# Value products of a token tile in one row, and a block compression in one row over four column strips

## The chip, the cores and the metric

The kernel runs on one core of a Trainium2 chip. The metric is the device time of one execution in microseconds; a time of a kernel is the median of several runs.

## What is computed

A decoder trunk of two layers on 256 tokens of width 1024, batch 1, all in fp32. A layer normalises its input, projects it to 5472 columns, mixes the tokens in two ways (NSA and DSA), gates and adds the two, projects back and adds the residual; a SwiGLU FFN with 2816 hidden columns follows. What touches the change, cut down:

```python
def _compress(kv, pos_emb, w1, b1, w2, b2):      # keys and values of NSA, 15 blocks of 32 tokens
    blocks = kv[:, idx] + pos_emb[:, None, :]
    blocks = ...reshape(bsz, n_cmp, groups, CMP_BLOCK * hd)      # 2048 long
    hidden = jax.nn.gelu(blocks @ w1 + b1)                       # w1: 2048 x 128
    return hidden @ w2 + b2

# NSA, 8 heads in 2 groups: compressed, selected and window attention, gated and added
o_c = p_c @ vc;  o_s = p_s @ v_slc;  o_w = p_w @ v_win
out = g[:, :, 0] * o_c + g[:, :, 1] * o_s + g[:, :, 2] * o_w
# DSA, 8 heads: softmax over the 64 tokens that an indexer chose
o = masked_softmax(q @ k.T * ATTN_SCALE, chosen) @ v
```

## The kernel before

The tokens lie in two tiles of 128 (`i` = 0 and 1). Tensor-engine instructions are issued through the Tile framework, which orders them when the program is built: a planner with a simulated timeline gives each engine its next instruction, the earliest of the program among those that are ready. `tc.manual_schedule` fixes the order of the instructions inside one block for an engine.

Weights come through `weights` (lines 155 to 167): a load of up to 512 KB on SP's queue into one of five raw buffers, a rounding to fp32r on the scalar engine (line 164, `hi`), a subtraction on the vector engine (line 165, `lo`), each into one of four pairs of buffers. `mul3` (lines 169 to 175) makes three fp32r products of them for each tile. These wide products have 512 (or 280, 292, 256) columns.

In a layer the order of the program is: projection of the indexer, its scores and top-k (lines 381 to 453); projections for NSA (458 to 494); the compression (497 to 548); projections of DSA's queries, keys and values (551 to 560); `nsa(0)`, `nsa(1)`, `dsa(0)`, `dsa(1)` (570 to 683); four projections of the gates, with a tanh into `gates` (691 to 694); the two branches, NSA's first (733 to 740); the output projection and the FFN. As the planner takes what is ready, the gates' projections and the first branch products also run between the attention's instructions.

The compression multiplies blocks of 32 columns (15 blocks of two groups, padded) with `w1`. Keys and values (`kind`) and the two halves of a block (`half`) make four sums of 8 products each, which lie in four strips of 32 partitions of one PSUM bank `hp` (`tile_position=(0, q)`). A strip's products come one behind the other (lines 508 to 518). The weights come in eight loads of 256 KB through three buffers `w1`; in layer 0 the first three wait for the first projection, by a copy into a corner of the buffer (`after`). `hp` is copied (line 520), its halves are added (522), and the GELU and second products follow.

`softmax` (287 to 312) takes two score banks of a step, and gives each its probabilities, transposed by the tensor engine (line 280) and copied into a buffer `pt` (line 281), of which there are five. `nsa(i)` goes over its heads in steps of `per = 2 - i` (two steps for tile 0, four for tile 1), `dsa(i)` in one and two steps. A step has two `pt` buffers. `values` (602 to 610 and 644 to 651) multiplies a step's `pt` with the values, into 64 partitions of the bank `yv` for each of two heads in turn; with `LAG = 1` it is called for a step once the next step's softmax is in the program. Behind the steps of `nsa(i)` the compressed values are added (line 634), and `y_out` (565 to 568) takes the bank out for the branches.

`gb` is a buffer of 5632 columns. It holds `gates` (columns 0 to 4095), and behind them `pji`, later `dkT` and `vbd`. The same memory (`bigB`) holds the low halves `hl` of the FFN's hidden values at the end of a layer.

Of the kernel before, what the change touches and what calls it, by code (L numbers as in the profile page):

```python
# [9 lines left out]
F32 = mybir.dt.float32  # L10
# [6 lines left out]
P = 128  # L17
# [10 lines left out]
TAKEN = -3e38  # L28
TOPK = 64
WARM = 11  # L30
LAG = 1
HALF = (slice(0, 64), slice(64, 128))
PTB = 5


C_KCMP, C_VCMP, C_KSLC, C_VSLC, C_KWIN, C_VWIN, C_NG = 512, 640, 768, 896, 1024, 1152, 1280
# [43 lines left out]
def hybrid_trunk(ctx: ExitStack, tc: tile.TileContext, a: dict, out: bass.AP):  # L80
# [272 lines left out]
    for l in range(DEPTH):  # L353
# [19 lines left out]
        qs = one.tile([P, 2, 4, SEQ], F32R, tag="qs", name="qs")  # L373
        ikT = carve(ga, 5168, P)
        gates = carve(gb, 0, NT, 2 * D)
        pji = carve(gb, 4096, NT, 648)
        dkT = carve(gb, 4096, 4, SEQ)
        vbd = carve(gb, 5120, 8, 64)
# [115 lines left out]
            nc.vector.tensor_scalar(eg[:, i], eg[:, i], 1.0, None, ALU.add)  # L494


        hp = sc_bank()
        for kind, nm in ((0, "cmpk"), (1, "cmpv")):
            blk = work.tile([P, 16, 32], F32, tag="pr", name="blk", bufs=8)
            blk4 = blk.rearrange("p m (g c) -> p m g c", g=2)  # L500
            nc.vector.memset(blk4[:, :, :, 15:16].rearrange("p m g c -> p (m g) c"), 0.0)
            pos = (R_KP, R_VP)[kind] + 16 * l
            for half in range(2):
                src = kvP[:, kind].rearrange("p g (c m) -> p m g c", m=8)[:, :, :, half:half + 15]
                po = cols[:, pos + half * 8:pos + half * 8 + 8].unsqueeze(2).broadcast_to((P, 8, 15))
                for g in range(2):
                    nc.vector.tensor_add(blk4[:, half * 8:(half + 1) * 8, g, 0:15], src[:, :, g], po)
            for half in range(2):
                q = 32 * (2 * half + kind)
                for mq in range(2):  # L510
                    r0 = half * 1024 + mq * 512
                    w1 = work.tile([P, 4, P], F32, tag="w1", name="w1", bufs=3)
                    if l == 0 and kind == 0 and half + mq < 2:
                        after(w1[:, 0, 0:1], pji[:, 0, 0:1])
                    nc.sync.dma_start(w1, a[nm + "_w1"][l, r0:r0 + 512].rearrange("(m p) h -> p m h", p=P))
                    for m in range(4):
                        nc.tensor.matmul(hp[q:q + 32, 0:P], blk[:, half * 8 + mq * 4 + m], w1[:, m],  # L517
                                         start=mq == 0 and m == 0, stop=mq == 1 and m == 3, tile_position=(0, q))
        hs = work.tile([P, P], F32, tag="hs", name="hs", bufs=1)
        nc.vector.tensor_copy(hs, hp[:, 0:P])  # L520
        hT = sc_bank()
# [48 lines left out]
        def nsa(i):  # L570
            tok = slice(i * P, (i + 1) * P)
            nk = P * (i + 1)

            cb = sc_bank()
            for r in range(4):
                nc.tensor.matmul(cb[:, r * 32:(r + 1) * 32], qT[:, r, tok], kcbd.rearrange("p g c -> p (g c)"),
                                 start=True, stop=True)
            pc = work.tile([P, 8, 16], F32, tag="pc", name="pc")
            m8 = small.tile([P, 8], F32, tag="cm", name="cm")
            s8 = small.tile([P, 8], F32, tag="cs", name="cs")  # L580
            bias = cst[:, K_CB + 16 * i:K_CB + 16 * i + 16].unsqueeze(1).broadcast_to((P, 8, 16))
            ok = cst[:, K_C01 + 16 * i:K_C01 + 16 * i + 16].unsqueeze(1).broadcast_to((P, 8, 16))
            nc.vector.tensor_add(pc, cb[:, 0:128].rearrange("p (h c) -> p h c", h=8), bias)
            nc.vector.tensor_reduce(m8, pc, AX.X, ALU.max)
            nc.vector.tensor_sub(pc, pc, m8.unsqueeze(2).broadcast_to((P, 8, 16)))
            nc.scalar.activation(pc, pc, AF.Exp, scale=0.125)
            nc.vector.tensor_mul(pc, pc, ok)
            nc.vector.tensor_reduce(s8, pc, AX.X, ALU.add)
            nc.vector.tensor_scalar_max(s8, s8, 1e-30)
            nc.vector.scalar_tensor_tensor(s8.rearrange("p (r g) -> p r g", g=2),  # L590
                                           eg[:, i, 0:8].rearrange("p (g r) -> p r g", g=2), 1.0,
                                           s8.rearrange("p (r g) -> p r g", g=2), ALU.mult, ALU.mult)
            nc.vector.reciprocal(m8, s8)
            nc.vector.tensor_mul(pc, pc, m8.unsqueeze(2).broadcast_to((P, 8, 16)))
            pct = work.tile([P, 1, P], F32, tag="pct", name="pct")
            transpose_into(pct, [pc.rearrange("p h c -> p (h c)")])


            per = 2 - i
            yn = yv_bank()  # L600

            def values(r0, pts):
                for r in range(r0, r0 + per):
                    for kind, vcol in ((0, C_VSLC - C0), (1, C_VWIN - C0)):
                        for b in range(i + 1):
                            for g in range(2):
                                nc.tensor.matmul(yn[g * 64:(g + 1) * 64, r * P:(r + 1) * P],  # L607
                                                 pj[:, b, vcol + g * 64:vcol + g * 64 + 64],
                                                 pts[g][:, ((r - r0) * 2 + kind) * (i + 1) + b],
                                                 start=r == 0 and kind == 0 and b == 0, stop=False)  # L610

            done = []
            for r0 in range(0, 4, per):
                pts = []
                sbs = [sc_bank() for _ in range(2)]
                outs = [[sb[:, n * 256 * (i + 1):(n + 1) * 256 * (i + 1)] for n in range(per)] for sb in sbs]
                for r in range(r0, r0 + per):
                    for g in range(2):
                        score(outs[g][r - r0], qs[:, g, r, tok],
                              [t[g][:, 0:i + 1].rearrange("p b t -> p (b t)") for t in (kh, kl)])  # L620
                for g in range(2):
                    segs = []
                    for o in outs[g]:
                        ov = o.rearrange("p (b k t) -> p k b t", b=i + 1, k=2)
                        segs += [ov[:, 0], ov[:, 1]]
                    gate = eg[:, i, 8:24].rearrange("p (k g r) -> p g r k", k=2, g=2)[:, g, r0:r0 + per]
                    pts.append(softmax(segs, causal(i), gate))
                done.append((r0, pts))
                if len(done) > LAG:
                    values(*done.pop(0))  # L630
            for d in done:
                values(*d)
            for r in range(4):
                nc.tensor.matmul(yn[:, r * P:(r + 1) * P], vbd[:, 2 * r:2 * r + 2].rearrange("p g d -> p (g d)"),  # L634
                                 pct[:, 0], start=False, stop=r == 3)
            y_out(yn, 0, tok)

        def dsa(i):
# [1 line left out]
            nk = P * (i + 1)  # L640
            per = 512 // nk
            yd = yv_bank()

            def values(p0, pts):
                for p in range(p0, p0 + per):
                    for b in range(i + 1):
                        for e in range(2):
                            v0 = (2 * p + e) * 64
                            nc.tensor.matmul(yd[e * 64:(e + 1) * 64, p * P:(p + 1) * P], dv[:, b, v0:v0 + 64],  # L649
                                             pts[e][:, (p - p0) * (i + 1) + b], start=p == 0 and b == 0,  # L650
                                             stop=p == 3 and b == i)

            done = []
            for p0 in range(0, 4, per):
                pts = []
                sbs = [sc_bank() for _ in range(2)]
                for p in range(p0, p0 + per):
                    outs = [sb[:, (p - p0) * nk:(p - p0 + 1) * nk] for sb in sbs]
                    if i == 0:
                        for e in range(2):  # L660
                            nc.tensor.matmul(outs[e], dqT[HALF[e], p, 0:P], dkT[HALF[e], p, 0:P], start=True, stop=True)
                    else:
                        for e in range(2):
                            score(outs[e], [dqs[:, z, p] for z in (e, 2 + e)], dks[:, e, p])
                for sb in sbs:
                    segs = sb.rearrange("p (h b t) -> p h b t", h=per, t=P)
                    pts.append(softmax([segs[:, h] for h in range(per)], dbias[i], None))
                done.append((p0, pts))
                if len(done) > LAG:
                    values(*done.pop(0))  # L670
            for d in done:
                values(*d)
            y_out(yd, 4, tok)

        for i in range(NT):
# [197 lines left out]
```

## Time and profile before

| | us |
|---|---|
| median of 3 runs | 821.17 (820.97 to 821.17) |
| the profiled execution, whole | 821.0 |
| its span in the profile | 819.2 |
| tensor engine busy (PE) | 810.9 (99%) |
| vector engine busy (DVE) | 549.5 (67%) |
| scalar engine busy (ACT) | 461.3 (56%) |
| mean rate of the DMA | 171 GB/s |

PE is the tensor engine's multiplication, PEld its weight load, which lies beside it. A matmul's record starts with its first column and lasts until its last result, so records overlap, and the distance from one start to the next is what a matmul costs in a row. SPq is the queue on which the loads are issued. A line such as `73.22 2.40 PE L517 ... x24` says that 24 instructions of line 517 started from 73.22 us on and that the last one ended 2.40 us later.

### The profile page before, as it was taken

To read this page: it belongs to the slowest core of one execution; us is meant where nothing else is said; L and a number is where in the kernel's file an instruction comes from. 1 tells how busy PE (TensorE), PEld (TensorE's weight loads), DVE (VectorE), ACT (ScalarE), POOL (GpSimd) and SP (SyncE) were. 2 spreads that over 40 slices of the span, in tenths; PEclk is the share of its full clock that TensorE was granted. 3 is DMA by queue.
4 is the path that set the end of the run, shared out by engine and by line. 5 is a ranking of instruction groups with operands and counts; after the bars stand their busy time and mean duration, and the time that the engine had idled before them with its cause. 6 is when DMAs were issued, how large, how long until landed. Compare 5 with 4: busy or idle time off the path is not lost.

```text
span 819.2 us, 12201 instructions
## 1 busy us (share of the span) xinstructions
PE 810.9 (99%) x4437; PEld 679.2 (83%) x4437; DVE 549.5 (67%) x1201; ACT 461.3 (56%) x791; POOL 8.4 (1%) x18
## 2 busy tenths in 40 slices
PE   8999999999999999999999999999999999999997
PEld 7887888888888888988898888888888888889886
DVE  5799668887665555554577994889776556546445
ACT  6866358773655445444467644778556445444433
POOL 0100000000000000000000000000000000000000
PEclk9999999999999999999999999999999999999999
DMA  8955754125475664576376564542345665547651
GB/s 275 343 165 168 218 172 138 52 81 180 152 231 164 196 183 152 169 241 193 102 214 191 170 207 142 153 129 78 128 134 175 206 192 183 182 119 231 202 177 52
DMA packets 76332, 140.09 MB, mean 171 GB/s; under 512 B 5056, under 2 KB 24512, under 8 KB 76272
## 3 DMA queue, kind: packets, MB, share of 16 engines
q1 hardware_dynamic: 76032, 138.59, 54.2%
q0 software_dynamic: 240, 0.72, 0.4%
q8 instruction: 35, 0.57, 0.3%
q14 instruction: 25, 0.20, 0.1%
HBM read 138.24 MB, written 1.05 MB: 170 GB/s over the span
## 4 chain that ended last, share of the span: by engine, by line
PE 98%; DMA 1%; SPq 0%; ACT 0%; DVE 0%; issue 0%; POOLq 0%; ACTq 0%
PE mm L175 26%; PE mm L173 26%; PE mm L174 26%; PE tr L280 3%; PE sc L335 2%; PE sc L517 2%; PE yv L607 2%; PE yv L175 2%; PE yv L174 2%; PE yv L173 1%; PE tr L798 1%; PE yv L649 1%; DMA raw<-w_in 1%; PE tr L234 1%; PE yv L634 1%; PE sc L174 0%
## 5 line engine op out<-in xcount | busy, mean ns | idle before, releaser
L165 DVE TENSOR_TENSOR lo<-raw,hi 128x1024 fp32r<-128x1024 f32 (+3 forms) x264 | 301.7, 1148 | 159.2 <-ACT hi L164 155.4
L164 ACT ACTIVATE hi<-raw 128x1024 fp32r<-128x1024 f32 (+3 forms) x264 | 262.2, 1000 | 189.3 <-PE mm L175 129.0
L174 PE MATMUL mm<-lo,ah 128*128 128x512 f32 (+3 forms) x850 | 318.9, 375 | 0.0
L175 PE MATMUL mm<-hi,al 128*128 128x512 f32 (+3 forms) x850 | 318.6, 376 | 0.0
L173 PE MATMUL mm<-hi,ah 128*128 128x512 f32 (+3 forms) x850 | 317.5, 379 | 0.0
L175 PEld LDWEIGHTS mm<-hi,al 128*128 128x128 f32 x850 | 159.8, 188 | 28.4 <-issue 1.5
L174 PEld LDWEIGHTS mm<-lo,ah 128*128 128x128 f32 x850 | 160.1, 188 | 26.8 <-issue 0.3
L173 PEld LDWEIGHTS mm<-hi,ah 128*128 128x128 f32 x850 | 159.7, 188 | 27.1 <-ACT hi L164 0.3
L300 ACT ACTIVATE pr<-pr,mx 128x128 f32<-128x128 f32 (+1 forms) x96 | 42.7, 448 | 12.4 <-DVE mx L297 12.1
L174 PE MATMUL mm<-lo,hh 128*128 128x512 f32 x126 | 49.3, 391 | 0.0
L175 PE MATMUL mm<-hi,hl 128*128 128x512 f32 x126 | 49.1, 390 | 0.0
L173 PE MATMUL mm<-hi,hh 128*128 128x512 f32 x126 | 48.7, 395 | 0.0
L803 DVE TENSOR_TENSOR hl<-tr,hh 128x512 fp32r<-128x512 f32 (+1 forms) x24 | 15.5, 647 | 36.5 <-ACT hh L802 36.5
L802 ACT ACTIVATE hh<-tr 128x512 fp32r<-128x512 f32 (+1 forms) x24 | 13.5, 562 | 45.4 <-PE tr L798 45.4
L175 PEld LDWEIGHTS mm<-hi,hl 128*128 128x128 f32 x126 | 23.7, 188 | 4.9
L174 PEld LDWEIGHTS mm<-lo,hh 128*128 128x128 f32 x126 | 23.7, 188 | 4.1
L173 PEld LDWEIGHTS mm<-hi,hh 128*128 128x128 f32 x126 | 23.7, 188 | 4.2
L309 DVE TENSOR_SCALAR pr<-pr,c 128x128 f32<-128x128 f32 (+1 forms) x96 | 24.7, 316 | 0.6
L297 DVE CUSTOM_DVE_ANT_0 pr<-sc,cst 128x128 f32<-128x128 f32 (+1 forms) x64 | 19.0, 353 | 6.3 <-PE sc L335 6.0
L280 PE MATMUL tr<-cst,pr 128*128 128x128 f32 x144 | 20.7, 273 | 0.0
L789 ACT ACTIVATE sg<-mm,rstd 128x512 f32<-128x512 f32 (+1 forms) x24 | 15.7, 654 | 8.8 <-PE mm L175 8.6
L281 ACT COPY pt<-tr 128x512 f32<-128x512 f32 x32 | 17.6, 584 | 4.4 <-PE tr L280 4.4
(247 smaller groups left out, 800.3 us busy)
## 6 DMA issues: line engine op xcount, KB each, us to landing
raw<-w_in SPq DMA_DIRECT2D x72, 512.0 KB, 3.7
raw<-w_ffn_down SPq DMA_DIRECT2D x44, 512.0 KB, 4.4
raw<-w_ffn_gate SPq DMA_DIRECT2D x40, 512.0 KB, 4.5
raw<-w_ffn_up SPq DMA_DIRECT2D x40, 512.0 KB, 4.3
raw<-w_out SPq DMA_DIRECT2D x16, 512.0 KB, 4.1
raw<-w_in SPq DMA_DIRECT2D x16, 292.0 KB, 3.7
raw<-w_branch_nsa SPq DMA_DIRECT2D x16, 256.0 KB, 3.9
raw<-w_branch_dsa SPq DMA_DIRECT2D x8, 512.0 KB, 3.7
```

Of the source, the lines that this page charges most:

```text
L164: nc.scalar.activation(hi[:, 0:kt * n], raw[:, 0:kt * n], AF.Copy)
L165: nc.vector.tensor_sub(lo[:, 0:kt * n], raw[:, 0:kt * n], hi[:, 0:kt * n].bitcast(F32))
L173: nc.tensor.matmul(dst, xh, wh, start=first, stop=False)
L174: nc.tensor.matmul(dst, xh, wl, start=False, stop=False)
L175: nc.tensor.matmul(dst, xl, wh, start=False, stop=last)
L280: nc.tensor.transpose(tp[:, k * P:(k + 1) * P], piece, ident)
L281: nc.any.tensor_copy(dst, tp[:, 0:len(parts) * P].rearrange("p (k t) -> p k t", t=P))
L297: nc.vector.tensor_tensor_reduce(pr[:, h].rearrange("p (b t) -> p b t", t=P), v, b3, -0.125, 3.4e38, ALU.add, ALU.min, accum_out=mx[:, h:h ...
L300: nc.scalar.activation(pr[:, h], pr[:, h], AF.Exp, bias=mx[:, h:h + 1], scale=-1.0, accum_out=sm[:, h:h + 1])
L309: nc.vector.tensor_scalar_mul(pr[:, h], pr[:, h], c[:, h:h + 1])
L335: nc.tensor.matmul(o, u, v, start=n == 0, stop=n == 1)
L517: nc.tensor.matmul(hp[q:q + 32, 0:P], blk[:, half * 8 + mq * 4 + m], w1[:, m], start=mq == 0 and m == 0, stop=mq == 1 and m == 3, tile_pos ...
```

## The change

The value products of a token tile no longer follow each step: they stand in one block of fixed order behind the last softmax of the tile, from the last head pair to the first, the two strips in turn. `LAG` goes, and `pt` has eight buffers. The compression's 32 products stand in one block of fixed order too, in which the four strips take turns. Its weights come in four loads of 512 KB into the memory of `gates`, which is written later in the layer; the `w1` buffers go.

```diff
-LAG = 1
-PTB = 5
+PTB = 8
...
         gates = carve(gb, 0, NT, 2 * D)
+        w1s = [gb[:, z * 1024:(z + 1) * 1024].rearrange("p (m h) -> p m h", h=P) for z in range(4)]
...
         hp = sc_bank()
-        for kind, nm in ((0, "cmpk"), (1, "cmpv")):
+        blks = []
+        for kind in range(2):
             blk = work.tile([P, 16, 32], F32, tag="pr", name="blk", bufs=8)
...
-            for half in range(2):
-                q = 32 * (2 * half + kind)
-                for mq in range(2):
-                    r0 = half * 1024 + mq * 512
-                    w1 = work.tile([P, 4, P], F32, tag="w1", name="w1", bufs=3)
-                    if l == 0 and kind == 0 and half + mq < 2:
-                        after(w1[:, 0, 0:1], pji[:, 0, 0:1])
-                    nc.sync.dma_start(w1, a[nm + "_w1"][l, r0:r0 + 512].rearrange("(m p) h -> p m h", p=P))
-                    for m in range(4):
-                        nc.tensor.matmul(hp[q:q + 32, 0:P], blk[:, half * 8 + mq * 4 + m], w1[:, m],
-                                         start=mq == 0 and m == 0, stop=mq == 1 and m == 3, tile_position=(0, q))
+            blks.append(blk)
+        strips = [(half, kind) for half in range(2) for kind in range(2)]
+        for (half, kind), w1 in zip(strips, w1s):
+            if l == 0:
+                after(w1[:, 0, 0:1], pji[:, 0, 0:1])
+            src = a[("cmpk_w1", "cmpv_w1")[kind]][l, half * 1024:(half + 1) * 1024]
+            nc.sync.dma_start(w1, src.rearrange("(m p) h -> p m h", p=P))
+        with tc.manual_schedule(engines={nc.tensor.engine}):
+            for m in range(8):
+                for (half, kind), w1 in zip(strips, w1s):
+                    q = 32 * (2 * half + kind)
+                    nc.tensor.matmul(hp[q:q + 32, 0:P], blks[kind][:, half * 8 + m], w1[:, m],
+                                     start=m == 0, stop=m == 7, tile_position=(0, q))
...
-            def values(r0, pts):
...
                 done.append((r0, pts))
-                if len(done) > LAG:
-                    values(*done.pop(0))
-            for d in done:
-                values(*d)
+            with tc.manual_schedule(engines={nc.tensor.engine}):
+                for n, (r, kind, b, g) in enumerate((r, kind, b, g) for r in range(3, -1, -1) for kind in range(2)
+                                                    for b in range(i + 1) for g in (1, 0)):
+                    r0, pts = done[r // per]
+                    vcol = (C_VSLC, C_VWIN)[kind] - C0 + g * 64
+                    nc.tensor.matmul(yn[g * 64:(g + 1) * 64, r * P:(r + 1) * P], pj[:, b, vcol:vcol + 64],
+                                     pts[g][:, ((r - r0) * 2 + kind) * (i + 1) + b], start=n < 2, stop=False)
...
-            def values(p0, pts):
...
                 done.append((p0, pts))
-                if len(done) > LAG:
-                    values(*done.pop(0))
-            for d in done:
-                values(*d)
+            with tc.manual_schedule(engines={nc.tensor.engine}):
+                for p in range(3, -1, -1):
+                    p0, pts = done[p // per]
+                    for b in range(i + 1):
+                        for e in (1, 0):
+                            v0 = (2 * p + e) * 64
+                            nc.tensor.matmul(yd[e * 64:(e + 1) * 64, p * P:(p + 1) * P], dv[:, b, v0:v0 + 64],
+                                             pts[e][:, (p - p0) * (i + 1) + b], start=p == 3 and b == 0,
+                                             stop=p == 0 and b == i)
```

## Rows read from the trace of the kernel before

**Rows 1.** The page, busy time of the tensor engine.

```profile
PE 810.9 (99%) x4437; PEld 679.2 (83%) x4437; DVE 549.5 (67%) x1201; ACT 461.3 (56%) x791; POOL 8.4 (1%) x18
```

**Rows 2.** The page, chain that ended last, by engine.

```profile
PE 98%; DMA 1%; SPq 0%; ACT 0%; DVE 0%; issue 0%; POOLq 0%; ACTq 0%
```

**Rows 3.** Windows, layer 0: busy us (x) PE, PEld, DVE, ACT, POOL; clock; DMA share; GB/s.

```profile
95.00:100.00 5.00, 5.00 (x27) 4.16 (x26) 1.61 (x3) 3.00 (x5) 0.00 (x0) 1.00 0.60 178
...
165.00:170.00 5.00, 5.00 (x42) 4.33 (x41) 5.00 (x27) 4.77 (x19) 0.00 (x0) 1.00 0.65 213
170.00:175.00 5.00, 5.00 (x42) 4.13 (x41) 5.00 (x20) 3.06 (x11) 0.00 (x0) 1.00 0.38 105
```

**Rows 4.** Instructions of lines 517 and 607: durations, first and last start, shapes.

```profile
L517 PE MATMUL sc<-w,blk x128: 272/273/297, 73.2 to 496.5; 128*32 128x128 f32 x128
...
L607 PEld LDWEIGHTS yv<-pt,ga x192: 132/137/137, 134.4 to 577.1; 128*64 128x64 f32 x192
L607 PE MATMUL yv<-pt,ga x192: 272/273/324, 134.4 to 577.2; 128*64 128x128 f32 x192
```

**Rows 5.** Timeline of the tensor engine around compression groups of layer 0: start, length.

```profile
72.90 0.40 PE L174 MATMUL mm<-lo,ah 128*128 128x512 f32 x1
73.22 2.40 PE L517 MATMUL sc<-w,blk 128*32 128x128 f32 x24
75.55 0.50 PE L175 MATMUL mm<-hi,al 128*128 128x512 f32 x1
...
82.76 0.40 PE L175 MATMUL mm<-hi,al 128*128 128x512 f32 x1
83.08 1.94 PE L517 MATMUL sc<-w,blk 128*32 128x128 f32 x16
84.95 0.66 PE L280 MATMUL tr<-cst,dq 128*128 128x128 f32 x4
...
90.46 0.39 PE L174 MATMUL mm<-lo,ah 128*128 128x512 f32 x1
90.69 0.39 PE L175 MATMUL mm<-hi,al 128*128 128x512 f32 x1
91.01 1.06 PE L517 MATMUL sc<-w,blk 128*32 128x128 f32 x8
92.00 0.50 PE L173 MATMUL mm<-hi,ah 128*128 128x512 f32 x1
92.33 0.40 PE L174 MATMUL mm<-lo,ah 128*128 128x512 f32 x1
```

**Rows 6.** Timeline of the tensor engine around value groups of layer 0.

```profile
164.50 0.39 PE L174 MATMUL mm<-lo,ah 128*128 128x512 f32 x1
164.81 1.09 PE L607 MATMUL yv<-pt,ga 128*64 128x128 f32 x16
165.84 1.21 PE L335 MATMUL sc<-dks,dqs 128*128 128x256 f32 x8
...
173.65 1.09 PE L607 MATMUL yv<-pt,ga 128*64 128x128 f32 x16
...
176.50 0.50 PE L173 MATMUL mm<-hi,ah 128*128 128x512 f32 x1
...
186.43 1.09 PE L649 MATMUL yv<-pt,ga 128*64 128x128 f32 x14
```

**Rows 7.** Waits of SP's queue: total us, times, longest.

```profile
SPq L515 <- PE sc L517: 8.4, 10, 1.6
```

**Rows 8.** Windows early in layer 0 and early in layer 1.

```profile
20.00:25.00 5.00, 5.00 (x26) 4.20 (x25) 3.65 (x4) 3.57 (x7) 0.00 (x0) 1.00 1.03 400
...
410.00:415.00 5.00, 5.00 (x40) 4.83 (x38) 4.59 (x14) 4.26 (x13) 0.55 (x1) 1.00 0.53 157
...
420.00:425.00 5.00, 5.00 (x36) 4.79 (x36) 3.71 (x5) 3.68 (x6) 0.00 (x0) 1.00 0.98 316
```

**Rows 9.** Timeline, the last FFN product of layer 0.

```profile
409.69 0.39 PE L175 MATMUL yv<-spare,hl 128*128 128x512 f32 x1
```

More of the change, by code (lines that the diff above doesn't have):

```diff
@@ L600, in nsa @@
             yn = yv_bank()
-            def values(r0, pts):
[L603 to L610, printed above, removed]
             done = []
@@ L642, in dsa @@
             yd = yv_bank()
-            def values(p0, pts):
[L645 to L651, printed above, removed]
             done = []
```

## The prediction

> **What bounds the kernel now.** I read the page's busy times first, then the chain of work that ended last. The tensor engine is busy 99% of the span and the chain lies on it for 98% [rows 1, 2]: whoever takes work from that engine gains it, as long as the other engines keep up. So I ask of each edit what it takes from the tensor engine, and then, in the windows of 5 us, whether something else is close to full. It is in one place: between 165 and 175 us the vector engine is busy all of the time [rows 3], while from 95 to 100 us it is busy a third of it [rows 3]. The granted clock is 1.00 (2.4 GHz) in all these windows, and the change leaves no gap that would lower it.
>
> Then the timeline of the tensor engine around the lines that change. A fp32 product makes two passes: line 517 has 64 products in the program and 128 matmul records, line 607 has 96 and 192 [rows 4]. What the reader is to see there is that these small products come in groups between wide matmuls, and that a group costs more than its passes.
>
> **Compression, before.** A layer has 64 passes in five groups, of 24, 8, 16, 8 and 8. In the group of 16 the passes, all to one strip of 32 columns, follow at (1.94 - 0.27) / 15 = 0.11 us, 0.27 being the duration of the last [rows 4, 5]. Two wide matmuls in a row start 0.23 us apart (90.46 to 90.69) [rows 5]; so the cost of a group is the time from the start before it to the start behind it, less 0.23, plus what the next step is longer than usual (0.33 instead of 0.23 behind the group of 8; 0.06 where transposes follow). That gives 24: 2.65 - 0.23 + 0.13 = 2.55 (the two steps behind it are longer there); 16: 2.19 - 0.23 + 0.06 = 2.02; 8: 1.31 - 0.23 + 0.10 = 1.18 [rows 5]. With three groups of 8 a layer pays 2.55 + 2.02 + 3 x 1.18 = 8.1 us. Of a group some 0.34 us is the change of shape: about 0.1 on the way in, 0.1 out, and the rest the longer first steps.
>
> **Compression, after.** One row of 64 passes, in which consecutive products go to four different strips. How many strips run at once is not in the trace for four. For two it is: 16 value passes that alternate between two strips take 1.09 us, that is (1.09 - 0.27) / 7 = 0.117 a step for eight steps of two [rows 6], and nothing is lost against one strip. So the bounds are four at once, 16 steps, which is the cost of the present group of 16, 2.0 us; and two at once, 32 steps, 2.0 + 16 x 0.11 = 3.8 us. I take four, as two showed no loss. The saving is 8.1 - 2.0 = 6.1 us a layer, **12.1 us** in all; by the other bound 4.3 a layer, 8.7 in all. The start flags, the bank and the sums are as before; the row waits for both blocks, whose additions are the same instructions.
>
> **Value products.** The passes stay, as does their step. Between the first group of a layer at 134.4 us and the last at 186.4 there are eleven groups [rows 4, 6]; after the change there are four rows. A group of 16 costs 1.34 - 0.23 + 0.10 = 1.21 us between a wide matmul and a score [rows 6], and its eight steps 8 x 0.109 = 0.87; the remaining 0.34 is what a merged group saves. Seven groups fewer: 2.4 us a layer, 4.9 in all.
>
> What this adds is a wait: the first product of a row, of the last head pair, waits for the last softmax of the tile, and everything behind it on the tensor engine waits too; `y_out` waits for the whole row. Three of the four groups of heads of tile 1 move from 151 to 165 us to the row's end. In their place come projections of the gates and the first branch matmuls, which are the only work without a softmax ahead. They already run out: from 173.65 to 176.50 there is no wide matmul, only the value group, the compressed values and transposes [rows 6]. In that stretch the vector engine is full [rows 3], so its chain sets the pace and the tensor engine would idle. The gain here is bounded by 4.9 us from above; from below by three groups of 1.2 us a layer that move to the end and leave idle time behind, 3.6 against the 2.4 saved, so 2.4 us lost in both layers. But each of these groups now stands in front of the next scores and delays them by its 1.0 us (164.81 to 165.84) [rows 6]; that goes, and shortens the chain. I take half of the upper bound, **2.5 us**. Eight transposed-probability buffers instead of five are what the row of tile 1 needs (four steps of two); the next tile's copies wait until that row is through, as they now wait for its last group.
>
> **Loads.** The bytes stay: eight loads of 256 KB become four of 512 KB a layer, 2 MB. Gone are the waits of the load queue for line 517, 8.4 us in ten waits [rows 7]; the tensor engine did not wait for data in those places, so they bring nothing. New is when the 2 MB come. In layer 0 all four wait for the first projection and come at once, 1.25 MB more than now, near a stretch with the DMA engines full at 400 GB/s [rows 8]: 3 us of transfer, which the prepared weights (five raw, four split) should cover; I take 0, at most 1. In layer 1 the gates' memory is the one that held the FFN's low halves, so the loads wait for the last FFN product, at 409.69 us [rows 9], where the queue turns to the loads of the first projection. Those windows have DMA shares of 0.53 and 0.98 [rows 8]; 2 MB at 400 GB/s are 5.2 us more. What stands behind the four loads on the queue is late by up to that; split weights in hand cover most of it. I take **1 us lost**, bounds 0 and 3. The corner copies rise from three to four, one column each, on a vector engine with room.
>
> **Sum.** 12.1 + 2.5 - 1.0 = 13.6 us. The profiled execution took 821.0 us (span 819.2 and 1.8 around it), 0.2 below the median of 821.2; 821.2 - 13.6 = **807.6 us**.
>
> **Rivals.**
> Two strips at once. If a pass cannot start before the one ahead of it in the program, the second pass of a product, which waits for the first, holds back the next strip, and only two overlap: 8.7 + 2.5 - 1.0 = 10.2 saved, 811.0 us. Against it: by such an order the 16 value passes would need eight steps from the first start to the last, and (1.09 - 0.27) leaves room for seven of 0.117 [rows 6]. The Trainium skill states this order (TensorE: Matmul & The Clock Gate, "What overlaps and what doesn't": matmuls start and end strictly in program order, and a weight load overlaps only a matmul of another row group); by it the sum is this rival's. The trace does not agree with the second half either: 16 loads of 137 ns lie within 1.09 us, though all strips here use the same rows [rows 4, 6]. Chance 0.14.
>
> The fillers run out. All that the value rows save comes back as idle time of the tensor engine, and 1 us a layer of the compression with it: 12.1 - 2.0 - 1.0 = 9.1, 812.1 us. For it stands the full vector engine at 165 to 175 us [rows 3]. Chance 0.11.
>
> The row is broken. The fixed order holds within the row, but the planner may still put other work between its products; each break costs 0.34 us. With three breaks in each of ten rows 10 us are gone: 817 to 818 us. Chance 0.04. If everything cancels, no change: 0.03.
>
> Slower. The chain of softmaxes on the vector and scalar engines sets the pace from the top-k on, and the tensor engine is full only because it is handed filler. Then all that it saves, 8.5 us a layer, turns to idle time, and the late rows lengthen the chain: 64 passes instead of 16 before `y_out` of tile 1 are 24 steps, 2.6 us, and 32 instead of 14 at the last row are 0.9, so 3.5 us a layer; with 1 us of loads 821.2 + 7.0 + 1.0 = 829 us. It becomes slower than before once less than half of the 8.5 us gets through (4.0 / 8.5 = 0.47). Against it stands the vector engine's third from 95 to 100 us [rows 3]: the chain can start earlier there. Chance 0.05.
>
> **How the numbers follow.** The forecast case has 0.63. Its cases and the first three rivals are faster by more than 0.2% (1.6 us, about what a measurement here can tell): 0.63 + 0.14 + 0.11 + 0.04 = 0.92; the same 0.03; slower 0.05. The range goes from all gains in full with no loss, 821.2 - 12.1 - 4.9 = 804.2, to two strips, no gain from the values and 3 us of late loads: 821.2 - 8.7 + 3.0 = 815.5.
>
> **What would show it.** Right: one group of 64 passes a layer on line 517's products with about 1.9 us from first start to the end (3.6 for two strips), four value rows a layer, no tensor-engine idle behind loads after 410 us. Wrong: tensor-engine waits on the vector engine between 150 and 180 us, waits on loads after 410, or compression passes still 0.11 us apart one by one.

## The result, and the profile after

The changed kernel takes 806.36 us (median of 4 runs, 806.26 to 806.85), the kernel before 821.07 us beside it (820.77 to 821.17): a ratio of 0.982 with a 95% interval of 0.981 to 0.983, 14.7 us faster. 807.6 was forecast. The profiled execution took 806.85 us whole, 0.5 above its median, with a span of 805.1.

The page's first line and the head of its chain, which answer to [rows 1, 2]:

```profile
PE 796.1 (99%) x4437; PEld 670.4 (83%) x4437; DVE 544.1 (68%) x1196; ACT 462.6 (57%) x797; POOL 8.4 (1%) x18
...
PE 97%; DMA 2%; ACT 0%; SPq 0%; DVE 0%; issue 0%; POOLq 0%; ACTq 0%
```

The tensor engine has the same 4437 matmul records and is busy 14.8 us less (810.9 before): the gain is cheaper records, not fewer. And the DMA has risen from 1% to 2% of the chain; that is the price, below.

The tensor engine's timeline around the compression of layer 0 (start, length, as in [rows 5]; line numbers are those of the changed kernel, 172 to 174 being `mul3`):

```profile
72.70 0.40 PE L173 MATMUL mm<-lo,ah 128*128 128x512 f32 x1
73.03 0.41 PE L523 MATMUL sc<-gb,blk 128*32 128x128 f32 x2
73.36 0.50 PE L174 MATMUL mm<-hi,al 128*128 128x512 f32 x1
73.70 0.39 PE L172 MATMUL mm<-hi,ah 128*128 128x512 f32 x1
73.93 0.40 PE L173 MATMUL mm<-lo,ah 128*128 128x512 f32 x1
74.25 1.95 PE L523 MATMUL sc<-gb,blk 128*32 128x128 f32 x62
76.13 0.50 PE L174 MATMUL mm<-hi,al 128*128 128x512 f32 x1
76.47 0.40 PE L172 MATMUL mm<-hi,ah 128*128 128x512 f32 x1
```

Five groups have become one of 62 passes, with a small one of two ahead. From the first start to the last the 62 take 1.95 - 0.27 = 1.68 us, 15.4 steps of 0.109: four passes to a step. But the row is broken behind its first product (two passes), and three wide matmuls stand in between. By the prediction's rule for the cost of a group, with a next step of 0.34 us behind each, the 62 cost 2.20 - 0.23 + 0.11 = 2.08 us and the two 0.66 - 0.23 + 0.11 = 0.54. Layer 1 has the same groups.

The value rows of layer 0, which answer to [rows 6]; there are no others in the layer:

```profile
130.18 1.97 PE L631 MATMUL yv<-pt,ga 128*64 128x128 f32 x32
...
161.11 3.71 PE L631 MATMUL yv<-pt,ga 128*64 128x128 f32 x64
...
170.15 1.09 PE L666 MATMUL yv<-pt,ga 128*64 128x128 f32 x16
...
178.41 1.97 PE L666 MATMUL yv<-pt,ga 128*64 128x128 f32 x32
```

Windows over the attention of layer 0, columns as in [rows 3]:

```profile
145.00:150.00 5.00, 5.00 (x33) 4.20 (x34) 4.93 (x22) 5.00 (x14) 0.00 (x0) 1.00 0.01 2
150.00:155.00 5.00, 5.00 (x29) 4.29 (x28) 5.00 (x17) 4.70 (x17) 0.00 (x0) 1.00 0.54 161
155.00:160.00 5.00, 5.00 (x31) 4.38 (x29) 5.00 (x28) 5.00 (x14) 0.00 (x0) 1.00 0.64 216
...
165.00:170.00 5.00, 5.00 (x33) 4.38 (x32) 1.38 (x2) 1.56 (x3) 0.00 (x0) 1.00 0.05 20
170.00:175.00 5.00, 5.00 (x39) 4.13 (x38) 1.81 (x2) 3.65 (x5) 0.00 (x0) 1.00 0.02 3
```

The full stretch of the vector engine has moved some 15 us to the front, and from 165 to 175 us it now works for a third of the time. The tensor engine is busy for 5.00 of every 5 us throughout, at a clock of 1.00 (2.4 GHz): the fillers did not run out.

Now the loads. The load queue's timeline early in layer 1, and the chain there (start, us, what):

```profile
401.66 0.37 SPq L518 DMA_DIRECT2D gb<-cmpk_w  x1
402.07 0.58 SPq L518 DMA_DIRECT2D gb<-cmpv_w  x1
402.75 0.65 SPq L161 DMA_DIRECT2D raw<-w_in  x1
403.44 0.84 SPq L518 DMA_DIRECT2D gb<-cmpk_w  x1
404.38 1.34 SPq L161 DMA_DIRECT2D raw<-w_in  x1
405.76 0.56 SPq L518 DMA_DIRECT2D gb<-cmpv_w  x1
```

```profile
406.42 8.78 DMA raw<-w_in
415.31 1.07 ACT hi L163
416.40 1.24 DVE lo L164
417.68 0.50 PE mm L173
```

Once the last FFN product (401.24 us) has read the memory, the compression's 2 MB go out among the loads of the first projection. The load of that projection behind them lands 8.78 us after its issue and is on the chain. The tensor engine's timeline shows what that costs:

```profile
413.75 0.30 PE L172 MATMUL mm<-hi,ah 128*128 128x292 f32 x1
414.22 0.40 PE L173 MATMUL mm<-lo,ah 128*128 128x292 f32 x1 [0.17 <-DVE lo L164]
...
415.67 0.29 PE L174 MATMUL mm<-hi,al 128*128 128x292 f32 x1
416.42 0.49 PE L172 MATMUL mm<-hi,ah 128*128 128x512 f32 x1 [0.45 <-ACT hi L163]
```

A step of this shape is 0.13 us; here two of them are 0.47 and 0.75, and from 416.42 to the chain's next matmul at 417.68 there are 1.26 instead of 0.23. Together they are about 2.0 us too long.

**Layer by layer.** The last FFN product of layer 0 starts at 409.69 before [rows 9] and at 401.24 after, that of layer 1 as follows (first line before, second after):

```profile
811.37 0.28 PE L175 MATMUL yv<-spare,hl 128*128 128x256 f32 x1
```

```profile
797.28 0.28 PE L174 MATMUL yv<-spare,hl 128*128 128x256 f32 x1
```

Layer 0 gains 8.5 us. Layer 1 was 401.7 long and is 396.0: it gains 5.6. The work is the same in both, so the 2.8 us between them point to the loads; a kernel below tries this.

### The profile page after: what moved, and what is told of

Same layout as the page of the kernel before. It is cut to its first block, busy times and chain, and to the rows that moved or that the text cites. A ratio compares the mean times of both kernels' runs of the same rounds, so it can differ in the third digit from the quotient of the medians.

```text
span 805.1 us, 12207 instructions
## 1 busy us (share of the span) xinstructions
PE 796.1 (99%) x4437; PEld 670.4 (83%) x4437; DVE 544.1 (68%) x1196; ACT 462.6 (57%) x797; POOL 8.4 (1%) x18
## 4 chain that ended last, share of the span: by engine, by line
PE 97%; DMA 2%; ACT 0%; SPq 0%; DVE 0%; issue 0%; POOLq 0%; ACTq 0%
PE mm L174 26%; PE mm L172 26%; PE mm L173 26%; PE tr L279 2%; PE sc L334 2%; DMA raw<-w_in 2%; PE yv L172 2%; PE yv L173 2%; PE yv L174 2%; PE yv L631 1%; PE tr L794 1%; PE yv L666 1%; PE tr L233 1%; PE sc L523 1%; PE yv L634 1%; PE sc L173 0%
## 5 line engine op out<-in xcount | busy, mean ns | idle before, releaser
L280 ACT COPY pt<-tr 128x512 f32<-128x512 f32 x36 | 19.8, 586 | 7.8 <-PE tr L279 7.0
```

What stands on the lines that cost most here:

```text
L280: nc.any.tensor_copy(dst, tp[:, 0:len(parts) * P].rearrange("p (k t) -> p k t", t=P))
```

## The experiments

Nine kernels, each against the kernel before on the same chip (821.1 to 821.3 us). Edits are shown against the changed kernel.

**Compression alone.** The value products as before, five `pt` buffers.

```diff
-PTB = 8
+LAG = 1
+PTB = 5
...
+                if len(done) > LAG:
+                    values(*done.pop(0))
```

> The compression of the changed kernel with the value products of the kernel before (five buffers, LAG). Theory: the two parts add up, and all that merging the value groups saves arrives. The compression then gives about 10.9 us less some 2.4 of late loads in layer 1, so 821.1 - 8.5 = 812.6 us; the value rows account for the other 6. Rival (the fillers run out, and the tensor engine gets the saved time back as idle): the value rows gave nothing, and this kernel takes what the changed one takes, 806.4 us.

Measured: 813.52 us, ratio 0.990 (0.989 to 0.992). So beside this compression the value rows are worth 813.52 - 806.36 = 7.2 us. But this is not the gain over the kernel before: here a layer has 13 value groups, where the kernel before has 11. Those of tile 0 of `nsa`:

```profile
120.61 0.43 PE L614 MATMUL yv<-pt,ga 128*64 128x128 f32 x2
126.00 1.09 PE L614 MATMUL yv<-pt,ga 128*64 128x128 f32 x16
130.47 1.09 PE L614 MATMUL yv<-pt,ga 128*64 128x128 f32 x14
```

Nine groups a layer more than after: 7.2 / 18 = 0.40 us a group, where 0.34 was read off. Against the kernel before, the value rows save seven groups a layer.

**Values in a fixed order, but from the first head pair to the last.** Is it the block of fixed order that makes the row, or the order within it?

```diff
-                for n, (r, kind, b, g) in enumerate((r, kind, b, g) for r in range(3, -1, -1) for kind in range(2)
-                                                    for b in range(i + 1) for g in (1, 0)):
+                for n, (r, kind, b, g) in enumerate((r, kind, b, g) for r in range(4) for kind in range(2)
+                                                    for b in range(i + 1) for g in range(2)):
```

(and the same in `dsa`, with its flags; the order of the two strips is turned as well)

> The changed kernel, but the value products of each block go from the first head pair to the last. Theory: the block fixes the order among its products and not that they stand together; with the earliest ready first, the planner starts them early again, in 13 pieces a layer for 4 rows. Nine more changes of shape at 0.34 us are 3.1 us a layer, 6 us in all: 812.5 us. Rival (the number of value groups costs nothing, as the vector engine sets the pace there): 806.4 us.

Measured: 813.6 us, 0.991 (0.989 to 0.992), the time of the kernel without value rows. Its value groups are 13 a layer again:

```profile
159.87 0.43 PE L631 MATMUL yv<-pt,ga 128*64 128x128 f32 x2
160.23 0.55 PE L279 MATMUL tr<-cst,pr 128*128 128x128 f32 x3
160.71 1.09 PE L631 MATMUL yv<-pt,ga 128*64 128x128 f32 x14
```

The block fixes the order of its products, not that nothing comes between them: a product whose operand is ready starts, and the next one's operand is not. From the last pair to the first, the operand made last is needed first; when it is there, all are, and the row runs through. The whole 7.2 us hang on that.

**The strips one behind the other.** One block, one row, but strip after strip.

```diff
-            for m in range(8):
-                for (half, kind), w1 in zip(strips, w1s):
+            for (half, kind), w1 in zip(strips, w1s):
+                for m in range(8):
```

> The changed kernel, but the one row goes through the four strips one behind the other. Theory: strips run at once only when they stand next to each other in the program, so the row takes 64 passes at 0.109 us less about 0.3 at each of three borders, 6.0 us for 1.8; with one break fewer at its start that is +3.9 us a layer, 814 us in all. Rival: what counted was that five groups became one, and the turn of the strips is worth nothing: 806 us.

**The strips two by two.**

```diff
-            for m in range(8):
-                for (half, kind), w1 in zip(strips, w1s):
+            for two in (0, 2):
+                for m in range(8):
+                    for (half, kind), w1 in zip(strips[two:two + 2], w1s[two:two + 2]):
```

> The changed kernel, but the row takes two strips in turn and then the other two. Theory (four at once): the row takes 32 steps of 0.109 less one border, 3.3 us for 1.8, so +1.5 us a layer and 809.4 us. Rival (a pass cannot start before the one ahead of it, so only two strips overlap in the changed kernel as well): the same as the changed kernel, 806.4 us.

Measured: 813.17 us, 0.990 (0.989 to 0.992), one by one, and 809.0 us, 0.985 (0.984 to 0.987), two by two. Their compression groups of layer 0, the first kernel's and then the second's:

```profile
73.44 5.96 PE L523 MATMUL sc<-gb,blk 128*32 128x128 f32 x64
```

```profile
73.34 0.41 PE L524 MATMUL sc<-gb,blk 128*32 128x128 f32 x2
...
74.56 3.28 PE L524 MATMUL sc<-gb,blk 128*32 128x128 f32 x62
```

First to last start: 5.69 us one by one, 3.01 two by two, 1.68 four by four. Two by two loses 809.0 - 806.36 = 2.6 us, and two layers of 3.01 - 1.68 make 2.7. One by one loses 6.8: two layers of 5.69 - 1.68 - 0.54 (this row is in one piece) make 6.9. So the four strips run at once, and what they save reaches the end in full.

**The old order of products with all weights early.** Eight loads of 256 KB into the gates' memory, no block; the value rows as after.

```diff
-                    w1 = work.tile([P, 4, P], F32, tag="w1", name="w1", bufs=3)
+                    w1 = w1s[half * 2 + kind][:, mq * 4:(mq + 1) * 4]
```

(against the kernel before, with `after` for every load of layer 0)

> The changed kernel with the compression's products in the order of the kernel before and in no fixed block, its weights in eight loads of 256 KB, all into the gates' memory and so with no wait for a free buffer. Theory: the five groups came from the products that waited for their weights through three buffers; with all weights there the planner puts the products together by itself, one group of 64 passes a layer, but strip behind strip, so it takes what the row with one strip after the other takes, 813.2 us. Rival: the fixed block is what keeps them together, and without it there are several groups a layer, 2 us more, 815 us.

Measured: 813.88 us, 0.992 (0.990 to 0.993).

```profile
73.27 5.96 PE L520 MATMUL sc<-gb,blk 128*32 128x128 f32 x64
```

Without any fixed order the 64 passes stand in one group: the five groups of before came from waiting for weights through three buffers. With the weights there, they run through, as slowly as in the row strip by strip. Memory for all the weights brings the merging; only the turns of the strips bring the rest.

**Loads of layer 1 later.** The copy into the corner, which is made in layer 0 alone, is made in layer 1 too, and waits for the NSA projection's output `pj`.

```diff
-            if l == 0:
-                after(w1[:, 0, 0:1], pji[:, 0, 0:1])
+            after(w1[:, 0, 0:1], pji[:, 0, 0:1] if l == 0 else pj[:, 0, 0:1])
```

> The changed kernel, but in layer 1 the four loads of the compression wait for the first evacuation of the NSA projection, some 25 us later, where the queue has weights in hand. Theory: in the changed kernel these 2 MB stand in front of the first projection's weights after the FFN, and the tensor engine waits 2.0 to 2.8 us for those; without that 806.4 - 2.4 = 804.0 us, and no step between wide products above 0.5 us after 400 us. Rival (layer 1 gains less than layer 0 for another reason, such as the planner's order): 806.4 us, the gaps stay or move. A second rival: the loads only move the wait to the next projection, 806 us.

Measured: 804.94 us, 0.980 (0.979 to 0.981). Layer 1 is 393.5 us long instead of 396.0, with no wait for data early in it; that is the price of the early loads in the changed kernel's profiled execution, 2.6 us. The time fell by 1.4 alone, since layer 0, whose code is the same, ended 0.7 later in this profiled execution (401.90) and the changed kernel's was 0.5 above its median. So the price is less than exact: it lies between 1.4, by the times, and 2.6, by the lengths of the layer.

**The strips of `kind` 1, the compressed values, first.**

```diff
-        strips = [(half, kind) for half in range(2) for kind in range(2)]
+        strips = [(half, kind) for half in range(2) for kind in (1, 0)]
```

> The changed kernel with the row's strips taken values first, so that its first product needs the block that is made last. Theory: the row is broken after its first product, because only the keys' block is there when it is planned; the broken-off product costs 0.55 us a layer against 0.05 in the row, so 0.45 us a layer and 0.9 in all: 805.5 us, one group of 64 passes a layer. Rival: the break costs nothing, 806.4 us.

Measured: 805.17 us, 0.980 (0.979 to 0.982).

```profile
74.36 1.95 PE L523 MATMUL sc<-gb,blk 128*32 128x128 f32 x64
```

The row is in one piece: the blocks of `kind` 1 are made last, and a row that begins with them finds all of them made. The break cost 806.36 - 805.17 = 1.2 us, by the sum 2 x 0.54 = 1.1. This kernel also gives a second price of the early loads, which it still has. Its layer 1 goes from 400.81 to 795.57, 394.8 us; with 0.54 for a break it would be 395.3, and that is 1.8 more than with the loads later.

**Both.**

> Both of the two edits before, later loads in layer 1 and the values' strips first. If both theories hold and add up: 806.4 - 2.4 - 0.9 = 803.1 us, faster than the kernel before and the changed one. If only the loads count, 804.0; if only the break, 805.5.

Measured: 805.09 us, 0.980 (0.979 to 0.982): a miss by 2 us. Neither part fails (row in one piece, no wait for loads), but layer 1 is 1.0 us longer than with the later loads alone (394.4 instead of 393.5), though its row, in one piece, saves 0.5: some 1.5 us are lost in it. The scores of `dsa(0)` there:

```profile
534.14 1.16 PE L651 MATMUL sc<-gb,ga 64*128 64x128 f32 x8
...
538.84 1.16 PE L651 MATMUL sc<-gb,ga 64*128 64x128 f32 x8
```

**Both, with the other order of strips in layer 0 alone.**

```diff
+        strips = [(half, kind) for half in range(2) for kind in ((1, 0) if l == 0 else (0, 1))]
+            after(w1[:, 0, 0:1], pji[:, 0, 0:1] if l == 0 else pj[:, 0, 0:1])
```

> The weight loads of both layers wait as in e5, and the strips of the values kind come first in layer 0 alone. Theory: in e7 the delayed loads and the unbroken row each gave their part, and about 1.0 us was given back because the other order of strips made the planner break up the scores of dsa(0) in layer 1. Then layer 0 is as in e7 (400.98 us up to its last FFN product) and layer 1 as in e5 (393.46 us long), 1.0 us under e7: 804.1 us, and the scores of dsa(0) in layer 1 cost about 1.1 us of steps instead of 2.2. Rival: the two gains share one cause and never add up; then about 805.0 us, as e5 to e7.

Measured: 803.96 us (803.8 to 805.8, 5 runs), 0.980 (0.978 to 0.981), 2.4 us under the changed kernel and the fastest here; the interval touches that of the changed kernel, and what carries the difference is the length of layer 1, 2.6 us shorter. Its compression row of layer 0 and its scores of `dsa(0)` in layer 1:

```profile
74.31 1.96 PE L522 MATMUL sc<-gb,blk 128*32 128x128 f32 x64
...
539.01 1.16 PE L651 MATMUL sc<-gb,ga 64*128 64x128 f32 x16
```

Layer 1 is back to 393.45, so it is the order of the strips in layer 1 that brought the loss. Eight passes alone take the 1.16 us that sixteen take here: in turn, the passes of a pair's two heads run side by side on the two halves of the 128 rows, two to a step, and in a group of eight each pass has a step of its own. The planner had torn them apart, and the second group is 1.1 us of steps. That is most of what "both" lost, not all. In its layer 1 the scores of `nsa` (`sc<-ks,qs`) stand in 11 groups instead of 8, those of `dsa(1)` (`sc<-dks,dqs`) in 6 instead of 3; whether the other 0.4 us are theirs was not tried.

## Why the prediction was right, and where its sizes were off

**In total** it was right, 1.2 us from the median, and each of the three terms has the sign forecast. Their errors are 1.1 us too much, 3.1 too little, and 0.4 to 1.6 of loss too little. They partly cancel, so that the sum came this close is in part luck.

**Compression, 12.1 forecast, 11.0 found.** Four strips at once was the right choice between the bounds; the row costs 2.08 us, where 2.0 was taken. The step that failed is "one row of 64 passes": 0.54 us a layer go to the break behind the first product, so a layer saves 8.1 - 2.62 = 5.5. The kernel with the compression alone bears this out in layer 0, where no load is waited for. Its last FFN product there starts at 405.18, so 409.69 - 405.18 = 4.5 us are gained, and 5.5 less two more value groups (0.8) is 4.7. The prediction had the break as a rival with three in each of ten rows; it came as one in each compression row, for a cause that the prediction had seen for the value rows alone (the operand that is made last stands first) and did not ask here.

**The rival of two strips** falls by the two kernels above. The row of [rows 6] which spoke against it decided rightly. In the row one by one the 64 passes take 5.69 / 0.109 = 52 steps from first to last start, not 63, although every strip's passes follow each other: passes of the next strip run beside the last of the one before.

The Trainium skill (TensorE: Matmul & The Clock Gate, "What overlaps and what doesn't") has matmuls start and end strictly in program order. The row one by one does not agree as far as the starts go: kept in order, they could save one step at each of the three changes of strip, and 11 are saved. Another page of the Trainium skill, TensorEngine Tiling (Array Packing), section "Theoretical Speedup", gives up to 4 times for 32 columns. The row in turns of four agrees: 62 passes in 15.4 steps.

**Values, 2.5 forecast, 5.6 found.** Fourteen groups fewer in the two layers at 0.40 us make 5.6, which is above what the prediction had as the most (4.9; its 14 groups at 0.34 are 4.8). Two things were wrong. The price of a group was 0.34, read from one place. And half of the gain was written off because the vector engine was full between 165 and 175 us. That row showed a full engine beside a tensor engine that was full too; it does not show that one waits for the other, and the windows after show that no such wait came. The chain of softmaxes began earlier and its full stretch moved along, by more than the 5.5 us that the compression saves: the first value group of layer 0, at 134.4 us before [rows 4], starts at 120.6 in the kernel with the compression alone. There the compression is through at 76.6 us, while the kernel before starts the last of its five groups here:

```profile
93.10 1.06 PE L517 MATMUL sc<-w,blk 128*32 128x128 f32 x8
```

The prediction had asked what the compression costs, not when it ends. A kernel with the value rows alone was not run; so whether the wait that it feared would have come without the earlier compression stays open. In the changed kernel the waits of the tensor engine name no softmax, only these:

```profile
PE tr L111 <- DVE warm L117: 1.2, 1, 1.2
PE mm L173 <- DVE lo L164: 0.9, 2, 0.8
PE mm L172 <- ACT hi L163: 0.5, 1, 0.5
PE sc L172 <- ACT hi L163: 0.3, 1, 0.3
```

**Loads, 1 us lost forecast, 2.6 found** in the profiled execution (1.4 by the times, 1.8 beside the unbroken row), within the bounds of 0 and 3. The mechanism and the place were right (layer 1, behind the last FFN product). What was mis-sized is the cover: the prediction let the split weights in hand hide all but 1 of 5.2 us of transfer, and here they hid half. Of the prediction's own signs of being wrong, "waits on loads after 410" is the one that came, and "no tensor-engine idle behind loads after 410 us", which it named as a sign of being right, did not fit the 1 us lost in its own sum. One suspect is cleared. In the load queue's waits the compression's first load stands 9.9 us at the head of the queue, in front of the projection's loads; but the queue of the last kernel, which has no such load there, stands still for 10.3 us too, for a raw buffer to come free (the changed kernel's row, then the last kernel's between 390 and 405 us):

```profile
SPq L518 <- PE yv L174: 9.9, 1, 9.9
```

```profile
SPq L161 <- DVE lo L164: 12.6, 3, 10.3
```

So that wait took no time from anyone; what is left is the bytes. From 410 us on, the columns as in [rows 3], the changed kernel and then the last one:

```profile
410.00:415.00 5.00, 4.83 (x36) 4.59 (x35) 1.02 (x2) 1.08 (x2) 0.00 (x0) 1.00 1.08 391
415.00:420.00 5.00, 3.78 (x19) 2.86 (x18) 3.55 (x7) 4.48 (x6) 0.00 (x0) 1.00 0.67 232
```

```profile
410.00:415.00 5.00, 5.00 (x39) 5.00 (x38) 3.19 (x4) 3.57 (x4) 0.00 (x0) 1.00 0.98 305
```

From 410 to 415 us the first moves more (391 against 305 GB/s), but what comes is not what the next product needs: the engines that split the weights (vector, scalar) work for 1.0 of 5 us instead of 3.2 and 3.6, and the tensor engine runs dry, mostly in the 5 us behind. Layer 0 paid nothing that can be seen, as forecast.

**The sum** is 11.0 + 5.6 - 2.6 = 14.0 us; the profiled executions differ by 821.0 - 806.85 = 14.15 (the medians by 14.7), and by layers it is 5.5 + 2.8 = 8.3 (8.5 found) and 8.3 - 2.6 = 5.7 (5.6 found).

## What to carry to other kernels

Small products of one kind belong in one row in which the column strips take turns, and the row should begin with the operand that is made last: a fixed order alone does not keep a row together. A buffer borrowed from another stage lets its load start only when that stage ends, among the next stage's first loads; a wait put in by hand, to a quiet stretch, left no wait for loads there. That a second engine is full in a window is no cost by itself: look whether the first one stands still there.

## What had not been expected of the hardware

Passes for different column strips do not wait for their turn in the program: one by one, the three changes of strip save 63 - 52 = 11 steps of 0.109 us, so in each some three to four passes of the next strip start beside the last ones of the strip before, without being written in turns. How far ahead the engine looks was not measured by itself.

A group of small products costs 0.40 us beside its passes (7.2 us for 18 groups), more than the 0.34 that its neighbours' longer steps show at one place; where the rest lies was not tried.
